# Opening loads, block-sum scalings and a row-factor power in another order

## The chip, the cores and the metric

The kernel runs on one core of one Trainium2 chip. The metric is the device time of one execution in microseconds (us), the median of several runs. TensorE (PE in the profile, its weight loads PEld) multiplies, VectorE (DVE), ScalarE (ACT) and GpSimd (POOL) work elementwise, SyncE (SP) and ScalarE issue the DMA transfers. Every engine takes its own instructions strictly in the order in which they were recorded and waits on semaphores for the others.

## The reference

One layer of a hybrid decoder trunk over 2048 positions and 16 meta tokens, 1024 channels wide. Everything is float32:

```python
h = concat([meta, x])                      # (1, 16 + 2048, 1024)
hn = rms_norm(h, norm1_g)                  # h * rsqrt(mean(h*h) + EPS) * g
proj = einsum('bld,de->ble', hn, w_in)     # 1024 -> 8 x 512
cx, cb, cc, cg, q, k, v, rg = split(proj, 8)
conv_out = short_conv_branch(cx, cb, cc, conv_w) * silu(cg)
ret = head_group_norm(retention_chunkwise(rotary(q), rotary(k), v), ret_norm_g)
mixed = concat([conv_out, ret * silu(rg)])
out = rms_norm(h + einsum('ble,ed->bld', mixed, w_out), final_g)[:, 16:]
```

The large work is the projection with w_in (1024 by 4096) and the one with w_out (1024 by 1024).

## The kernel before

**Tiling.** Positions are taken in two rounds (r = 0, 1) of 1024. A round's x stands transposed in 16 tiles of 128 channels by 512 positions, named by k (0 to 7, eight slices of channels) and j (0, 1, two halves of the positions). Eight units follow each other in a round: four convolution groups and four retention heads, each with two sets of four weight tiles ("ra", 128x512 each).

**Split products.** A float32 operand is split into a high part (rounded to a short float32 form) and a low part (the rest): ScalarE writes the high part (`mh` of a tile of x, `wh` of a weight tile), VectorE subtracts it for the low part (`ml`, `wl`). A product is three matmuls of 512 columns: high by high, high by low, low by high. `split` (line 107) does it; with a gain factor ScalarE's line is L113 and VectorE's L114, without it L110 and L122.

**Seven products for eight.** Most units use a scheme with seven block products (`quad`, L232): the weights go in as sums of the four blocks (`stationary`, line 134, whose sums GpSimd makes: L119, L122, L122, L149), x as sums of its four blocks (`block_sums`, line 177: L188 on ScalarE scales x tiles by the gain in place, L185 on VectorE, L122 on GpSimd). The first unit runs before these sums exist, so it multiplies plainly (`quad_plain`, L289), a contraction step k at a time: six matmuls for each tile of x (two weight tiles by three parts), with weight tiles 0 and 2 for k = 0 to 3 and tiles 1 and 3 for k = 4 to 7.

**The opening.** ScalarE's queue loads the gain and a first piece (128 of 512 columns, all that step k = 0 needs) of weight tiles 0 and 2 (L927). SP's queue loads x tile 0, then the remaining 384 columns of both weight tiles (L975), then x tiles 1 to 3, weight tiles 1 and 3, and the rest of x. Ten warm-up matmuls (L941) run before the first product. `begin` (line 968) splits the pieces (L984, L985).

**The row factors.** The norm's factor of each position is a power of the row's mean square: 16 half-row tiles are loaded (L363), ScalarE squares and sums them (L403), VectorE makes the variance (L119, L302), GpSimd raises it to -1/2 (`rsqrt_mean`, L305), VectorE puts it on a diagonal (L310), and TensorE spreads it over partitions (L336). This happens for the 512 positions of j = 0 and again for those of j = 1 while the first unit runs. Its results scale the first unit's outputs (L530).

**What sets the order.** The framework takes the program as written, estimates times, and records each engine's instructions in the order in which its estimate starts them. `tc.issue_after(ins)` keeps what stands inside from being recorded ahead of `ins`. Tiles come from rings of slots ("ra": 8), and a load waits until its slot is free. A DMA's landing is told on one of eight semaphores in turn, so a ninth transfer is issued when the first has landed.

Of the kernel before, what the change touches and what calls it, by code (L numbers as in the profile page):

```python
# [78 lines left out]
def hybrid_trunk(ctx: ExitStack, tc: tile.TileContext, t, out: bass.AP, chunk_decay):  # L79
# [27 lines left out]
    def split(hi, lo, src, scale=None, eng=nc.vector):  # L107

        if scale is None:
            nc.scalar.copy(out=hi, in_=src)  # L110
            sub(eng, lo, src, hi.bitcast(F32))
            return
        nc.scalar.mul(hi, src, scale)  # L113
        nc.vector.scalar_tensor_tensor(  # L114
            out=lo, in0=src, scalar=scale, in1=hi.bitcast(F32), op0=ALU.mult, op1=ALU.subtract
        )
# [14 lines left out]

    summed = [None]

    def stationary(blocks):
# [10 lines left out]
        w = [parts(a11), parts(a12)]  # L145
        add(nc.gpsimd, s1, a21, a22)
        sub(nc.gpsimd, a21, a11, a21)
# [14 lines left out]

    def moving(load, scale=None, after={}):


        m = [[] for _ in range(8)]
        blocks = []
        for j in range(2):
            for half in range(2):
                for kt in range(KH):  # L170
                    k = half * KH + kt
                    blocks.append(load(k, j))
                    parts(m, BLOCK[half][j], kt, blocks[-1], scale(k) if scale else None)
                    after.get((j, k), lambda: None)()
        return m, blocks
# [122 lines left out]
    def rsqrt_mean(r, total):  # L298

        n, w = total.shape  # L300
        v = small.tile([P, CH], F32, name="rs_v", tag="rs_v", bufs=4)
        nc.vector.tensor_scalar(  # L302
            out=v[:n, :w], in0=total, scalar1=1.0 / D, scalar2=EPS, op0=ALU.mult, op1=ALU.add
        )
        nc.gpsimd.tensor_tensor(out=r, in0=v[:n, :w], in1=neg_half[:n, :w], op=ALU.pow)  # L305
        return v[:n, :w]
# [106 lines left out]
    def load_x(r):  # L413
        def load(k, j):
            a = gen("x")[:, :HB]
            nc.sync.dma_start(a, t["xT"][r, j, k])
            return a
# [273 lines left out]
    def head(h, r, m, rot_t, f, turning, blocks, ahead, sums, first=(), between=((), idle, idle)):  # L691
# [5 lines left out]
        k, v, late = [None, None], [None, None], []  # L697
        rot = meta_table(h) if blocks[1] else None
        tables = [rot_t[:, :, j * HB : (j + 1) * HB] for j in range(2)]
# [225 lines left out]
    opening = {n: raw() for n in (0, 2)}  # L925
    for n, a in opening.items():
        nc.scalar.dma_start(a[:, PIECES[0]], t["w_in"][2 * NG, n][:, PIECES[0]])  # L927
    make_identity(nc, ident)
# [27 lines left out]
    for r in range(NR):  # L956
# [7 lines left out]
        if r == 0:  # L964
            w = [None] * 4
            loads = w_loads(2 * NG)

            def begin(half):
                if half:
                    for n in (1, 3):  # L970
                        w[n] = plain_part(n, loads[n], FIRST_W)
                    return
                for n, a in opening.items():
                    w[n] = a, operand(FIRST_W, n)
                    nc.sync.dma_start(a[:, PIECES[1]], t["w_in"][2 * NG, n][:, PIECES[1]])  # L975
                done = []
                for cs in PIECES:
                    with ExitStack() as behind:
                        for ins in done:
                            behind.enter_context(tc.issue_after(ins.ins))  # L980
                        for n, a in opening.items():
                            hi, lo = w[n][1]
                            done = [
                                nc.scalar.copy(out=hi[:, cs], in_=a[:, cs]),  # L984
                                nc.vector.tensor_tensor(  # L985
                                    out=lo[:, cs], in0=a[:, cs], in1=hi[:, cs].bitcast(F32), op=ALU.subtract
                                ),
                            ]

            m, b = moving(  # L990
                load_x(r), gain_of, {(0, 0): lambda: begin(0), (0, KH - 1): lambda: begin(1), (0, KT - 1): normalise_meta}
            )
            first = [[p for a, p in w]]
            blocks = None, meta_products([a for a, p in w])
            first.append(plain_parts(w_loads(2 * NG + 1)))
            load_tables()
            nc.sync.dma_start(cols, t["cols"])
            t3 = [a[:, i * HB : (i + 1) * HB] for a in (row_tile("t3", 1) for _ in range(2)) for i in range(2)]
            t1 = [brief("t1") if n < BRIEF else sb.tile([P, HB], F32, name="t1", tag="tc", bufs=COPIES) for n in range(KH)]
            for kt in range(KH):  # L1000
                b11, b21, b12, b22 = (b[n * KH + kt] for n in range(4))
                block_sums(b11, b12, b22, b21, t1[kt], t3[kt], gain_of(kt), gain_of(KH + kt), nc.gpsimd)
                parts(m, 2, kt, b22)
                parts(m, 6, kt, b21)
            for _ in row_factors(0, f):
                pass
            nc.sync.dma_start(causal, t["causal"])
            nc.sync.dma_start(conv_w, t["conv_w"])
            nc.sync.dma_start(ret_g, t["ret_norm_g"])

# [93 lines left out]
```

## Time and profile before

| | |
|---|---|
| median of 3 runs | 871.72 us (871.09 to 872.45) |
| profiled execution, device time | 872.54 us |
| its span, first to last instruction | 870.7 us |
| instructions in the trace | 12707 |
| granted TensorE clock | 0.999 |
| bytes read from HBM, written | 90.91 MB, 25.17 MB |

Times in the trace count from the first instruction. A row of the timeline has a start, a duration, engine, line, operation, tiles written and read, shape, a count where equal instructions follow each other, and in brackets how long the engine was idle before it and what ended that. A row of the table by stretches has, for each engine, busy us and the number of instructions, then the granted clock, the share of the DMA engines and GB/s. Durations of neighbours overlap by about 0.1 us on ScalarE and VectorE, because they are pipelined.

### The profile page before, as it was taken

To read this page: it belongs to the slowest core of one execution; us is meant where nothing else is said; L and a number is where in the kernel's file an instruction comes from. 1 tells how busy PE (TensorE), PEld (TensorE's weight loads), DVE (VectorE), ACT (ScalarE), POOL (GpSimd) and SP (SyncE) were. 2 spreads that over 40 slices of the span, in tenths; PEclk is the share of its full clock that TensorE was granted. 3 is DMA by queue.
4 is the path that set the end of the run, shared out by engine and by line. 5 is a ranking of instruction groups with operands and counts; after the bars stand their busy time and mean duration, and the time that the engine had idled before them with its cause. 6 is when DMAs were issued, how large, how long until landed. Compare 5 with 4: busy or idle time off the path is not lost.

```text
span 870.7 us, 12707 instructions
## 1 busy us (share of the span) xinstructions
PE 856.9 (98%) x4216; PEld 704.6 (81%) x4216; DVE 707.0 (81%) x1194; ACT 498.5 (57%) x899; POOL 395.0 (45%) x286
## 2 busy tenths in 40 slices
PE   8999999999999999999999999999999999999996
PEld 6878887878787878788888888888888887888885
DVE  6889988888897977989789898988767799655553
ACT  8675548383845554848383747553333565555553
POOL 0653332322246644352233333355746555677773
PEclk9999999999999999999999999999999999999999
DMA  9624236373656633845254645637122583555431
GB/s 332 224 81 97 74 78 166 105 174 107 136 194 184 202 98 97 311 150 145 61 137 141 130 161 121 206 109 218 49 77 81 179 317 133 168 171 175 152 134 73
DMA packets 127218, 129.51 MB, mean 149 GB/s; under 512 B 58352, under 2 KB 75568, under 8 KB 127152
## 3 DMA queue, kind: packets, MB, share of 16 engines
q1 hardware_dynamic: 126576, 128.30, 49.2%
q8 instruction: 33, 0.54, 0.3%
q10 hardware_dynamic: 576, 0.40, 0.1%
q14 instruction: 33, 0.27, 0.1%
HBM read 90.91 MB, written 25.17 MB: 133 GB/s over the span
## 4 chain that ended last, share of the span: by engine, by line
PE 82%; DVE 5%; ACT 4%; issue 2%; DMA 2%; SPq 0%; POOLq 0%; POOL 0%; ACTq 0%; DVEq 0%
PE pj L232 71%; PE pj L289 3%; DVE ml L122 2%; PE ms L818 2%; PE ms L807 2%; PE ms L817 2%; PE ms L794 2%; DMA t<-sums_w 1%; PE ms L452 1%; ACT wh L110 1%; DVE wl L122 1%; ACT v L762 1%; ACT v L765 1%; ACT tc L239 1%; DMA x<-in_xT 1%
## 5 line engine op out<-in xcount | busy, mean ns | idle before, releaser
L232 PE MATMUL pj<-mh,wl 128*128 128x512 f32 x1008 | 397.0, 394 | 2.6 <-ACT tc L239 2.5
L232 PE MATMUL pj<-mh,wh 128*128 128x512 f32 x1008 | 393.0, 390 | 0.0
L232 PE MATMUL pj<-ml,wh 128*128 128x512 f32 x1008 | 392.8, 390 | 0.0
L110 ACT CAST wh<-ra 128x512 fp32r<-128x512 f32 x216 | 133.8, 620 | 249.4 <-PE pj L232 199.6
L122 DVE TENSOR_TENSOR wl<-ra,wh 128x512 fp32r<-128x512 f32 x216 | 190.1, 881 | 45.7 <-ACT wh L110 43.9
L232 PEld LDWEIGHTS pj<-mh,wl 128*128 128x128 f32 x1008 | 189.3, 188 | 46.3 <-ACT tc L239 5.5
L232 PEld LDWEIGHTS pj<-mh,wh 128*128 128x128 f32 x1008 | 189.2, 188 | 39.6
L232 PEld LDWEIGHTS pj<-ml,wh 128*128 128x128 f32 x1008 | 189.4, 188 | 37.7
L119 POOL TENSOR_TENSOR sa<-ra 128x512 f32<-128x512 f32 x36 | 52.6, 1460 | 99.3 <-DMA ra<-in_w_in 34.3
L122 POOL TENSOR_TENSOR ra<-sa,ra 128x512 f32<-128x512 f32 x36 | 53.0, 1472 | 91.8 <-DVE wl L122 88.8
L149 POOL TENSOR_TENSOR ra<-ra 128x512 f32<-128x512 f32 x36 | 60.2, 1672 | 48.4 <-issue 38.5
L122 POOL TENSOR_TENSOR ra<-ra 128x512 f32<-128x512 f32 x36 | 56.9, 1580 | 50.2 <-PE ms L452 27.9
L239 ACT COPY tc<-pj 128x512 f32<-128x512 f32 x108 | 62.7, 581 | 0.1
L289 PE MATMUL pj<-mh,mh 128*128 128x512 f32 x128 | 50.7, 397 | 1.2 <-ACT mh L113 0.7
L289 PE MATMUL pj<-mh,ml 128*128 128x512 f32 x128 | 50.0, 390 | 1.0 <-DVE ml L122 1.0
L289 PE MATMUL pj<-ml,mh 128*128 128x512 f32 x128 | 48.0, 392 | 0.0
L887 DVE TENSOR_TENSOR yo<-pj,yo 128x512 f32<-128x512 f32 (+1 forms) x33 | 22.1, 674 | 31.8 <-PE pj L232 23.4
L592 POOL TENSOR_TENSOR c<-c,rr 128x512 f32<-128x512 f32 x14 | 25.5, 1820 | 25.6 <-DVE c L633 16.9
L830 POOL TENSOR_TENSOR rp<-rs,neg_half 128x4 f32<-128x4 f32 x16 | 18.9, 1184 | 39.2 <-DVE rs L119 39.1
L893 POOL TENSOR_TENSOR z<-yo,final_g 128x512 f32<-128x512 f32 x16 | 26.9, 1680 | 18.5 <-DVE yo L887 18.5
L110 ACT CAST wh<-sa 128x512 fp32r<-128x512 f32 x36 | 22.3, 619 | 18.1 <-PE pj L232 17.7
L119 POOL TENSOR_TENSOR yo<-yo,tc 128x512 f32<-128x512 f32 x18 | 28.6, 1589 | 8.8 <-ACT tc L239 8.8
(151 smaller groups left out, 1202.6 us busy)
## 6 DMA issues: line engine op xcount, KB each, us to landing
ra<-in_w_in SPq DMA_DIRECT2D x126, 256.0 KB, 2.8
x<-in_xT SPq DMA_DIRECT2D x48, 256.0 KB, 4.9
w<-in_w_out SPq DMA_DIRECT2D x32, 256.0 KB, 4.3
ra<-mixed SPq DMA_DIRECT2D x32, 256.0 KB, 2.7
yo<-in_x SPq DMA_DIRECT2D x32, 256.0 KB, 4.9
ra<-in_x SPq DMA_DIRECT2D x16, 256.0 KB, 3.4
mixed<-c SPq DMA_DIRECT2D x16, 256.0 KB, 2.5
mixed<-qg SPq DMA_DIRECT2D x16, 256.0 KB, 2.4
```

What stands on the lines that cost most here:

```text
L110: nc.scalar.copy(out=hi, in_=src)
L119: eng.tensor_tensor(out=out, in0=a, in1=b, op=ALU.add)
L122: eng.tensor_tensor(out=out, in0=a, in1=b, op=ALU.subtract)
L149: summed[0] = nc.gpsimd.tensor_tensor(out=a12, in0=a12, in1=a11, op=ALU.subtract)
L232: nc.tensor.matmul(bank, a[:, ks], b, start=first and kt == 0 and n == 0, stop=kt == KH - 1 and n == 2, skip_group_check=not first,)
L239: copied[0] = nc.scalar.copy(out=c, in_=bank)
L289: nc.tensor.matmul(banks[i], a[:, ks], b, start=half + kt + n == 0, stop=half == 1 and kt == KH - 1 and n == 2,)
L592: eng.tensor_tensor(out=out, in0=a, in1=b, op=ALU.mult)
L794: nc.tensor.matmul(up[:, cs], kd[:, cs], vj[:, cs], start=True, stop=True)
L830: nc.gpsimd.tensor_tensor(out=rp, in0=rs, in1=neg_half.rearrange("p (c a) -> p c a", a=1), op=ALU.pow)
L887: last[0] = nc.vector.tensor_tensor(out=y[:, cs], in0=pp[:, cs], in1=y[:, cs], op=ALU.add)
L893: nc.gpsimd.tensor_tensor(out=ys[i][j], in0=y, in1=final_g[:, j * HB : (j + 1) * HB], op=ALU.mult)
```

## The change

The change has four parts. (1) The first piece of weight tile 2 moves from ScalarE's queue to SP's, right behind x tile 0, then comes x tile 1, then the rest of both weight tiles; the splits of these pieces are ordered between those of x tiles 0, 1 and 2. (2) The block sums are recorded only after the split of x tile 7, so the scalings of x tiles 0 to 3 (L188, now L194) move behind it. (3) Later loads and the meta table are ordered behind the x loads. (4) In the first call of `stationary`, the weight sum on GpSimd is ordered behind the row-factor power of j = 1.

```diff
-        nc.scalar.mul(hi, src, scale)
+        scaled[0] = nc.scalar.mul(hi, src, scale)
...
         w = [parts(a11), parts(a12)]
-        add(nc.gpsimd, s1, a21, a22)
+        with tc.issue_after(powered.pop().ins) if powered else nullcontext():
+            add(nc.gpsimd, s1, a21, a22)
...
-    def moving(load, scale=None, after={}):
+    def moving(load, scale=None, after={}, behind={}):
...
-                    blocks.append(load(k, j))
-                    parts(m, BLOCK[half][j], kt, blocks[-1], scale(k) if scale else None)
+                    with ExitStack() as order:
+                        for ins in behind.get((j, k), lambda: ())():
+                            order.enter_context(tc.issue_after(ins.ins))
+                        blocks.append(load(k, j))
+                        parts(m, BLOCK[half][j], kt, blocks[-1], scale(k) if scale else None)
...
-        nc.gpsimd.tensor_tensor(out=r, in0=v[:n, :w], in1=neg_half[:n, :w], op=ALU.pow)
+        power = nc.gpsimd.tensor_tensor(out=r, in0=v[:n, :w], in1=neg_half[:n, :w], op=ALU.pow)
+        if n == P and w == CH and len(powers) < NR:
+            powers.append(power)
+            powered[:] = [power]
...
-    for n, a in opening.items():
-        nc.scalar.dma_start(a[:, PIECES[0]], t["w_in"][2 * NG, n][:, PIECES[0]])
+    nc.scalar.dma_start(opening[0][:, PIECES[0]], t["w_in"][2 * NG, 0][:, PIECES[0]])
...
+            def piece(at):
+                cs = PIECES[at]
                 for n, a in opening.items():
+                    if n or at:
+                        with tc.issue_after(fetched[0].ins):
+                            fetched[0] = nc.sync.dma_start(a[:, cs], t["w_in"][2 * NG, n][:, cs])
+                with tc.issue_after(scaled[0].ins):
+                    for n, a in opening.items():
...
+                        cast = nc.scalar.copy(out=hi[:, cs], in_=a[:, cs])
...
+            after = {
+                (0, 0): lambda: pieces.append(piece(0)),
+                (0, 1): lambda: pieces.append(piece(1)),
+                (0, KH - 1): rest_of_tiles,
+                (0, KT - 1): lambda: (pieces.append(scaled[0]), meta_behind()),
+            }
+            m, b = moving(load_x(r), gain_of, after, {(0, 1): lambda: pieces[0], (0, 2): lambda: pieces[1]})
...
+                    with tc.issue_after(pieces[2].ins):
+                        block_sums(b11, b12, b22, b21, t1[kt], t3[kt], gain_of(kt), gain_of(KH + kt), nc.gpsimd)
```

What it makes of the recorded order is shown at three places. In names, `mh00` to `mh03` and `mh10` to `mh13` are the high parts of x tiles 0 to 7, `mh20` to `mh23` those of the first set's weight tiles 0 to 3.

ScalarE at the start, before, from the first split on:

```order
L113 ACTIVATE mh00_123<-x_121,gain_69 128x512
L984 CAST mh20_127<-ra_94 128x128
L984 CAST mh22_130<-ra_95 128x128
L984 CAST mh20_127<-ra_94 128x384
L984 CAST mh22_130<-ra_95 128x384
L188 ACTIVATE x_121<-x_121,gain_69 128x512
L113 ACTIVATE mh01_143<-x_141,gain_69 128x512
L113 ACTIVATE mh02_149<-x_147,gain_69 128x512
L113 ACTIVATE mh03_155<-x_153,gain_69 128x512
L110 CAST mh21_161<-ra_159 128x512
L188 ACTIVATE x_141<-x_141,gain_69 128x512
```

The same place after the change, with the first piece of tile 2 now on SP's queue:

```order
L113 ACTIVATE mh00_122<-x_120,gain_69 128x512
L992 CAST mh22_131<-ra_95 128x128
L992 CAST mh20_127<-ra_94 128x128
L113 ACTIVATE mh01_137<-x_135,gain_69 128x512
L992 CAST mh20_127<-ra_94 128x384
L992 CAST mh22_131<-ra_95 128x384
L113 ACTIVATE mh02_149<-x_147,gain_69 128x512
L113 ACTIVATE mh03_155<-x_153,gain_69 128x512
L110 CAST mh21_161<-ra_159 128x512
L110 CAST mh23_167<-ra_165 128x512
L113 ACTIVATE mh10_173<-x_171,gain_69 128x512
```

Tile 1's split has moved ahead of the weights' rest, and no L188 stands among the splits; all four come behind `mh13`.

GpSimd around the second 128x4 power, before:

```order
L122 TENSOR_TENSOR t3_315<-x_254,x_147 128x512
L122 TENSOR_TENSOR t3_315<-x_260,x_153 128x512
L119 TENSOR_TENSOR sa_747<-ra_717,ra_719 128x512
L305 TENSOR_TENSOR rc_442<-rs_v_443,neg_half_73 128x4
L122 TENSOR_TENSOR ra_717<-ra_713,ra_717 128x512
```

and after:

```order
L122 TENSOR_TENSOR t3_315<-x_254,x_147 128x512
L122 TENSOR_TENSOR t3_315<-x_260,x_153 128x512
L311 TENSOR_TENSOR rc_442<-rs_v_443,neg_half_73 128x4
L119 TENSOR_TENSOR sa_747<-ra_717,ra_719 128x512
L122 TENSOR_TENSOR ra_717<-ra_713,ra_717 128x512
```

The power (L305, now L311) and the sum of two weight tiles have changed places.

VectorE around the diagonal that waits for this power (L310), before; `wl_749` and `wl_753` are low parts of the next unit's first two weight tiles, `ml63` belongs to the block sums:

```order
L122 TENSOR_TENSOR ml62_356<-x_183,mh62_355 128x512
L302 TENSOR_SCALAR rs_v_443<-ss_420 128x4
L122 TENSOR_TENSOR wl_749<-ra_713,wh_748 128x512
L383 TENSOR_TENSOR ev_456<-cols_75,rs_v_443 128x16
L122 TENSOR_TENSOR wl_753<-ra_715,wh_752 128x512
L122 TENSOR_TENSOR ml63_369<-x_189,mh63_368 128x512
L310 TENSOR_TENSOR rot_446<-ident_70,rc_442 128x512
L374 TENSOR_TENSOR rc2_452<-rc_442 128x4
```

and after:

```order
L308 TENSOR_SCALAR rs_v_443<-ss_420 128x4
L392 TENSOR_TENSOR ev_456<-cols_75,rs_v_443 128x16
L122 TENSOR_TENSOR ml62_356<-x_183,mh62_355 128x512
L319 TENSOR_TENSOR rot_446<-ident_70,rc_442 128x512
L383 TENSOR_TENSOR rc2_452<-rc_442 128x4
L122 TENSOR_TENSOR wl_749<-ra_713,wh_748 128x512
L122 TENSOR_TENSOR ml40_698<-t3_314,mh40_697 128x512
L385 TENSOR_TENSOR vk_454<-cols_75,rc2_452 128x16
L122 TENSOR_TENSOR wl_753<-ra_715,wh_752 128x512
L122 TENSOR_TENSOR ml63_369<-x_189,mh63_368 128x512
```

The diagonal (now L319) has moved ahead of both weight subtractions and of `ml63`. Behind these rows the order on VectorE, ScalarE and GpSimd is the same in both kernels as far as the weight pair that the prediction ends at, and from there on.

75 lines of the change are left out of this document (34 added, 41 removed).

## The prediction

> **What bounds the kernel now.** I read the page's busy shares first, then the chain that ended last by engine, then the table of busy time in stretches of 5 us, then TensorE's waits in the first 130 us.
>
> ```profile
> PE 856.9 (98%) x4216; PEld 704.6 (81%) x4216; DVE 707.0 (81%) x1194; ACT 498.5 (57%) x899; POOL 395.0 (45%) x286
> PE 82%; DVE 5%; ACT 4%; issue 2%; DMA 2%; SPq 0%; POOLq 0%; POOL 0%; ACTq 0%; DVEq 0%
> ...
> 0.00:5.00 5.00, 4.01 (x11) 1.53 (x11) 0.70 (x3) 2.44 (x4) 0.78 (x8) 1.00 0.60 188
> 5.00:10.00 5.00, 3.80 (x16) 2.57 (x15) 3.91 (x9) 4.47 (x9) 0.00 (x0) 1.00 0.91 329
> 10.00:15.00 5.00, 5.00 (x37) 3.77 (x35) 3.71 (x8) 5.00 (x10) 0.00 (x0) 1.00 1.06 394
> ...
> 50.00:55.00 5.00, 4.15 (x44) 2.53 (x43) 4.07 (x9) 4.33 (x11) 1.80 (x2) 1.00 0.00 0
> 55.00:60.00 5.00, 5.00 (x23) 4.12 (x23) 5.00 (x7) 1.73 (x5) 4.84 (x3) 1.00 0.00 0
> 60.00:65.00 5.00, 4.90 (x22) 3.76 (x22) 5.00 (x7) 3.10 (x6) 3.32 (x4) 1.00 0.19 51
> ...
> PE ms L336 <- DVE rot L310: 0.8, 1, 0.8
> PE pj L289 <- ACT mh L113: 0.7, 1, 0.7
> PE pj L289 <- ACT mh L984: 0.6, 1, 0.6
> ```
>
> TensorE is busy 98% of the span, so only its holes are worth anything, and the change touches the first 63 us. There it stands still at three places: 1.2 us in 5 to 10 us (waits of 0.6 and 0.7 for ScalarE), 0.8 us at 52 us (waits for VectorE's L310), and 0.1 us in 60 to 65 us. In that last stretch VectorE is full (5.00 of 5.00), and from 55 us on. Keep this: there are two clocks running side by side, and the later one counts.
>
> **The opening.** Engine rows in order of time:
>
> ```profile
> 4.81 0.52 PE L289 MATMUL pj<-mh,mh 128*128 128x512 f32 x1
> ...
> 5.53 1.13 ACT L984 CAST mh<-ra 128x128 fp32r<-128x128 f32 x3 [0.77 <-DMA ra<-in_w_in]
> ...
> 5.88 0.50 PE L289 MATMUL pj<-mh,mh 128*128 128x512 f32 x1 [0.55 <-ACT mh L984]
> ...
> 6.56 0.72 ACT L188 ACTIVATE x<-x,gain 128x512 f32<-128x512 f32 x1
> ...
> 7.19 1.93 ACT L113 ACTIVATE mh<-x,gain 128x512 fp32r<-128x512 f32 x3
> ...
> 7.95 0.50 PE L289 MATMUL pj<-mh,mh 128*128 128x512 f32 x1 [0.65 <-ACT mh L113]
> ...
> 10.67 0.72 ACT L188 ACTIVATE x<-x,gain 128x512 f32<-128x512 f32 x1
> ...
> 11.30 0.71 ACT L113 ACTIVATE mh<-x,gain 128x512 fp32r<-128x512 f32 x1
> ...
> 12.06 0.19 PEld L289 LDWEIGHTS pj<-mh,mh 128*128 128x128 f32 x1 [0.15 <-ACT mh L113]
> ...
> x<-in_xT SPq DMA_DIRECT2D x1, 256.0 KB, 5.6
> ...
> 57.27 5.44 PE pj L232 x24
> ```
>
> A contraction step k is six L289 products, 0.227 us apart (24 of the same shape take 5.44 us in the chain's piece at 57.27), so 1.36 us. Before: step 0 begins at 4.81, step 1 at 7.95, step 4 at 12.06. The change lets the second weight's first piece land beside the first's, so the wait at 5.88 should go; it takes the four block-sum scalings (L188, 0.72 each) from between the splits and puts them behind x tile 7; and it puts x tile 1 ahead of the weights' rest. Without the scaling at 6.56, tile 1's split starts by 6.56 and step 1 by 7.3 even if nothing landed earlier; with the earlier landing, about 6.3. Added: one issue of 64 KB on SP, taken from ScalarE's queue; the bytes in front of every later tile are the same.
>
> But step 4 needs x tile 4. Its load is issued at 5.13 (the row is the DMA view's, for the stretch from 5.0 to 5.3 us) and lands 5.6 us later, at 10.7; the split takes 0.71, so step 4 cannot begin before about 11.5, against 12.06. **Term: 0.5 us**, bounds 0 (a landing 0.5 later) and 0.6. The other 1.1 us won before it turn into a new wait in front of step 4. From there the moved scalings stand behind tile 7, at 13.4 (four splits 0.64 apart from 10.8) to 16.0 on ScalarE, and tile 8 is split at 16.0 to 16.7, while TensorE comes to it at 11.5 + 4 x 1.36 = 16.9. This cover is 0.2 us thick; without it TensorE waits as much as it is short, and the slack found below takes that up.
>
> **The power ahead of the weight sum.** Rows of the second place:
>
> ```profile
> 24.37 13.91 SPq L363 DMA_DIRECT2D ra<-in_x  x16
> ...
> 44.55 0.63 ACT L403 ACTIVATE ra<-ra 128x512 f32<-128x512 f32 x1
> ...
> 36.52 1.03 POOL L305 TENSOR_TENSOR rc<-rs_v,neg_half 128x4 f32<-128x4 f32 x1 [4.40 <-DVE rs_v L302]
> ...
> 46.43 0.16 DVE L302 TENSOR_SCALAR rs_v<-ss 128x4 f32<-128x4 f32 x1
> ...
> 48.52 1.29 POOL L119 TENSOR_TENSOR sa<-ra 128x512 f32<-128x512 f32 x1 [3.45 <-PE pj L289]
> 49.78 1.48 POOL L305 TENSOR_TENSOR rc<-rs_v,neg_half 128x4 f32<-128x4 f32 x1
> ...
> 51.29 0.69 DVE L310 TENSOR_TENSOR rot<-ident,rc 128x512 f32<-128x512 f32 x1 [0.93 <-POOL rc L305]
> ...
> 50.80 0.39 PE L289 MATMUL pj<-ml,mh 128*128 128x512 f32 x1
> 52.04 0.70 PE L336 MATMUL ms<-rot,ones 128*128 128x512 f32 x1 [0.85 <-DVE rot L310]
> ...
> 62.33 0.39 PE L232 MATMUL pj<-mh,wh 128*128 128x512 f32 x1
> 62.81 0.47 PE L232 MATMUL pj<-mh,wl 128*128 128x512 f32 x1
> ```
>
> The variance is ready at 46.6, yet the power starts at 49.78, because the sum ahead of it in GpSimd's queue waits until 48.52. TensorE issues its last product at 50.80 and is free at 51.03; it gets L336 at 52.04: **1.0 us** lost. In the new order the power runs at about 46.6. (The last square, at 44.55, moves one or two places of some 0.6 us back on ScalarE, to about 45.4, but the variance no longer stands behind a 0.6 us split of VectorE, so I keep 46.4.) The power takes 1.03 to 1.48 us (its two 128x4 instances, at 36.52 and 49.78), L310 starts at 47.7 to 48.1, and L336 is ready before TensorE comes to it. That wait is gone.
>
> TensorE alone would then reach its product with the third weight pair (62.81) earlier by 0.5 + 1.0 + 0.25 (the hole in front of 62.81: the last issue is 62.33, the next was due at 62.56) = **1.75 us**, at 61.05.
>
> **What is late next.** That product reads a low part that VectorE makes last:
>
> ```profile
> 51.29:62.67 11.38, 11.38 (x17) 1.00 0.00 0
> ...
> 48.63 1.74 DVE L122 TENSOR_TENSOR ml<-x,mh 128x512 fp32r<-128x512 f32 x1 [0.31 <-ACT mh L110]
> ...
> 53.87 3.09 DVE L122 TENSOR_TENSOR ml<-t,mh 128x512 fp32r<-128x512 f32 x5
> ...
> 54.45 3.66 POOL L122 TENSOR_TENSOR ra<-ra 128x512 f32<-128x512 f32 x1 [3.20 <-DVE u L530]
> 56.88 0.15 DVE L491 COPY carry<-ms 128x2 f32<-128x2 f32 x1
> 56.95 1.72 DVE L530 TENSOR_TENSOR u<-u,rr 128x512 f32<-128x512 f32 x1
> ...
> 61.99 0.68 DVE L122 TENSOR_TENSOR wl<-ra,wh 128x512 fp32r<-128x512 f32 x1
> ```
>
> From L310 to the end of that subtraction VectorE has no idle time: 11.38 busy of 11.38. In the new order L310 goes ahead of two weight subtractions and a tile's (the order on VectorE, above), 3 x 0.61 us (five take 3.09) = 1.83 more behind it. A GpSimd add that gets its operands in between stretches the VectorE instruction beside it by 1.05 to 1.1 us (1.74 at 48.63, 1.72 at 56.95, where 0.6 to 0.7 is usual); back-to-back subtractions keep it out instead (3.66 at 54.45, let in at the small copy at 56.88). In the new order the weight sum becomes ready at about 48.5, when VectorE has just started its closed run. If it is kept out until the copy, three stretches remain in the run as before (11.38 + 1.83 = 13.2): from 47.7 to 48.1 the subtraction ends at 60.9 to 61.3 and TensorE goes on at 61.05 to 61.4. **Shift 1.4 to 1.75; I take 1.5**, since the row at 54.45 shows the same situation. If it gets in at once, 1.1 more: 62.0 to 62.4, shift 0.3 to 0.7.
>
> The Trainium skill bears on this in "SBUF — State Buffer", section "SBUF: two separate sides": the port pair that VectorE and GpSimd share is an exclusive lock held for a whole instruction, taken by whichever starts first. Read as a hand-over after each instruction, it gives the second case; the trace agrees on the exclusion, but at 54.45 GpSimd waited through five instructions, not one.
>
> Behind 62.81 the order of all engines is as before, and waits there are relative to what TensorE and VectorE have done, so the shift stays until the end.
>
> **Sum.** The profiled execution is 872.54 us (span 870.7 and 1.8 around it), 0.8 above the median 871.72 and just outside the three runs. 872.54 - 1.5 = 871.0; from the median it would be 870.2. If some of that 0.8 is in the stall at 52 us, there is less to win in other runs; no row tells, so I go halfway: **870.6 us**.
>
> **Rivals.**
> - The sum gets in at once (shift 0.3 to 0.7): 871.0 to 872.2. For it: 48.63; against it: 54.45. Chance 0.28.
> - TensorE's full 1.75, from the median: 869.9. For it: VectorE's early estimate (60.9) lies under 61.05. Against: the closed run leaves 0.1 us. Chance 0.20.
> - Slower: the power late. L310 now stands in front of the two weight subtractions, and the first product with them waits if the power does. The power hangs on 16 loads of rows (L363, from 24.37 on), whose slots are freed by VectorE and ScalarE work that the change reorders. Each us of lateness beyond a power ending at 49.5 (62.67 less 13.2) is a us lost; with it ending at 51.4 the time is 873.5. That asks for the last square 3.3 us later than 45.4; the order moves it by about 0.9. Chance 0.07.
> - The forecast itself, shift 1.4 to 1.7, from the median or from the profiled time: 870.0 to 871.1. Chance 0.45.
>
> **Range and chances.** 0.2% is 1.74 us, about what a measurement of this kernel can tell from no change: below 869.98 is faster, above 873.46 slower. The range runs from 869.2 (full shift, a run at the low end) to 872.2 (the sum gets in at once). Faster 0.25 (the full shift and the lower end of the forecast), same 0.68, slower 0.07.
>
> **What would show it.** Right: no wait at 5.88; step 4 at about 11.5 with a new wait in front of it; the power at 46 to 47 on GpSimd ahead of the sum; L336 without a wait; and a larger wait than 0.1 in front of the third weight pair's product, ended by VectorE, at 61 to 61.5. Wrong: step 4 earlier than 11.3 (tile 4 landed earlier), the power later than 48, VectorE idle inside the run after L310, or a new wait behind 63 us.

## The result, and the profile after

| | median of 13 runs | profiled execution | its span |
|---|---|---|---|
| kernel before | 872.24 us (871.09 to 874.87) | 872.54 us | 870.7 us |
| changed kernel | 874.79 us (872.91 to 877.05) | 874.20 us | 872.4 us |

The ratio is 1.0027, with a 95% interval of 1.0019 to 1.0035: the change makes the kernel about 2.4 us slower. Forecast was 870.6, with 0.07 for slower.

TensorE's waits between 4 and 70 us of the changed kernel (operation, what it waited for, total, times, longest):

```profile
PE pj L238 <- DVE wl L122: 2.6, 1, 2.6
PE pj L295 <- ACT mh L992: 0.6, 2, 0.4
```

Lines have moved: L289 is now L295, L232 is L238, L310 is L319, L336 is L345, L305 is L311, L403 is L412, L530 is L539. The wait for the diagonal is gone from this execution, as was wanted. In its place stands one of 2.6 us for VectorE at the third weight pair. Rows in order of time around it:

```profile
45.49 0.61 ACT L110 CAST mh<-x 128x512 fp32r<-128x512 f32 x1
46.12 0.59 ACT L553 COPY cb<-pj 128x512 f32<-128x512 f32 x1
46.60 0.63 ACT L412 ACTIVATE ra<-ra 128x512 f32<-128x512 f32 x1
...
47.87 1.57 POOL L311 TENSOR_TENSOR rc<-rs_v,neg_half 128x4 f32<-128x4 f32 x1 [2.79 <-DVE rs_v L308]
49.76 1.54 POOL L119 TENSOR_TENSOR sa<-ra 128x512 f32<-128x512 f32 x1 [0.32 <-DMA ra<-in_w_in]
52.64 1.74 POOL L122 TENSOR_TENSOR ra<-ra 128x512 f32<-128x512 f32 x1 [1.33 <-DVE vk L385]
...
49.48 0.69 DVE L319 TENSOR_TENSOR rot<-ident,rc 128x512 f32<-128x512 f32 x1 [0.92 <-POOL rc L311]
50.08 1.24 DVE L383 TENSOR_TENSOR rc<-rc 128x4 f32<-128x4 f32 x1
...
53.14 1.79 DVE L122 TENSOR_TENSOR ml<-x,mh 128x512 fp32r<-128x512 f32 x1
54.85 1.78 DVE L539 TENSOR_TENSOR cb<-cb,rr 128x512 f32<-128x512 f32 x1
56.55 1.79 DVE L539 TENSOR_TENSOR u<-u,rr 128x512 f32<-128x512 f32 x1
58.26 3.09 DVE L122 TENSOR_TENSOR ml<-t,mh 128x512 fp32r<-128x512 f32 x5
...
63.14 0.68 DVE L122 TENSOR_TENSOR wl<-ra,wh 128x512 fp32r<-128x512 f32 x1
...
60.96 0.39 PE L238 MATMUL pj<-mh,wh 128*128 128x512 f32 x1
63.97 0.47 PE L238 MATMUL pj<-mh,wl 128*128 128x512 f32 x1 [2.62 <-DVE wl L122]
```

Read it from the end. TensorE came 1.37 us earlier than before (last issue at 60.96 instead of 62.33), but goes on 1.16 later (63.97 instead of 62.81), 0.14 after VectorE's low part. That low part is the last of a closed run which starts with the diagonal at 49.48 and has no hole, by VectorE's busy time in that stretch:

```profile
49.48:63.83 14.35, 14.35 (x20) 1.00 0.01 5
```

It was 11.38 before. Four of its instructions are stretched, one for each weight sum of GpSimd (a 128x4 one to 1.24 by the sum at 49.76; three to 1.79 by the others); before there were three. The diagonal itself waits 0.92 for the power, which starts late since the last square stands at 46.60: the copy of a product at 46.12 and a split are ahead of it on ScalarE, though the last row had landed at 45.43. That landing is itself late. The load of the last row, from the view of the tile `ra`, before and after (its duration in ns and its start, then the us from its issue to its landing):

```profile
L363 SPq DMA_DIRECT2D ra<-in_x x1: 382/382/382, 37.9 to 37.9; - x1
DMA to landing us min/median/max: 6.2/6.2/6.2
...
L372 SPq DMA_DIRECT2D ra<-in_x x1: 382/382/382, 39.4 to 39.4; - x1
DMA to landing us min/median/max: 6.0/6.0/6.0
```

Issued at 37.91 and 39.42, the row landed at 44.08 before and at 45.43 now, and its square followed 0.47 and 1.17 us behind. So of the 2.05 us by which the square is later (44.55 and 46.60), 1.35 come from the load and 0.7 from the order on ScalarE.

Of the 1.7 us between the two spans, 1.16 to 1.2 are there from 64 us on, 0.36 come at 297 us (a wait of 0.2 for VectorE and a slower restart), 0.1 at 742 us. The medians lie 2.55 apart, so some 0.8 us of that is not in this pair of profiles.

### The profile page after: what moved, and what is told of

It is laid out like the page before. It is cut to its first block, busy times and chain, and to the rows that moved or that the text cites. A ratio compares the mean times of both kernels' runs of the same rounds, so it can differ in the third digit from the quotient of the medians.

```text
span 872.4 us, 12711 instructions
## 1 busy us (share of the span) xinstructions
PE 857.2 (98%) x4216; PEld 704.5 (81%) x4216; DVE 708.2 (81%) x1194; ACT 498.8 (57%) x899; POOL 397.0 (46%) x286
## 3 DMA queue, kind: packets, MB, share of 16 engines
q1 hardware_dynamic: 126720, 128.37, 49.5%
## 4 chain that ended last, share of the span: by engine, by line
PE 85%; DVE 5%; ACT 4%; DMA 3%; issue 2%; POOL 0%; SPq 0%; POOLq 0%; ACTq 0%; DVEq 0%
PE pj L238 71%; PE pj L295 6%; PE ms L828 2%; PE ms L817 2%; PE ms L827 2%; PE ms L804 2%; DVE ml L122 1%; DMA ra<-in_x 1%; DVE wl L122 1%; PE ms L461 1%; DMA ra<-in_w_in 1%; ACT wh L110 1%; DVE ml L114 1%; ACT v L775 1%; ACT v L772 1%
## 5 line engine op out<-in xcount | busy, mean ns | idle before, releaser
L238 PE MATMUL pj<-mh,wl 128*128 128x512 f32 x1008 | 397.2, 394 | 5.4 <-DVE wl L122 2.8
L238 PE MATMUL pj<-mh,wh 128*128 128x512 f32 x1008 | 393.0, 390 | 0.0
L238 PE MATMUL pj<-ml,wh 128*128 128x512 f32 x1008 | 392.8, 390 | 0.0
L238 PEld LDWEIGHTS pj<-mh,wl 128*128 128x128 f32 x1008 | 189.3, 188 | 49.3 <-ACT tc L245 5.1
L238 PEld LDWEIGHTS pj<-mh,wh 128*128 128x128 f32 x1008 | 189.2, 188 | 39.7
L238 PEld LDWEIGHTS pj<-ml,wh 128*128 128x128 f32 x1008 | 189.3, 188 | 37.8
L119 POOL TENSOR_TENSOR sa<-ra 128x512 f32<-128x512 f32 x36 | 52.9, 1470 | 93.9 <-DMA ra<-in_w_in 38.2
L152 POOL TENSOR_TENSOR ra<-ra 128x512 f32<-128x512 f32 x36 | 60.2, 1672 | 48.8 <-issue 38.8
L122 POOL TENSOR_TENSOR ra<-ra 128x512 f32<-128x512 f32 x36 | 55.0, 1529 | 48.7 <-PE ms L461 28.0
L295 PE MATMUL pj<-mh,ml 128*128 128x512 f32 x128 | 50.2, 392 | 1.0 <-DVE ml L122 1.0
L295 PE MATMUL pj<-mh,mh 128*128 128x512 f32 x128 | 49.7, 392 | 0.7 <-ACT mh L992 0.6
L295 PE MATMUL pj<-ml,mh 128*128 128x512 f32 x128 | 48.2, 396 | 0.0
L119 POOL TENSOR_TENSOR yo<-yo,tc 128x512 f32<-128x512 f32 x18 | 28.8, 1602 | 9.2 <-ACT tc L245 9.2
L601 POOL TENSOR_TENSOR c<-c,tc 128x512 f32<-128x512 f32 x14 | 24.2, 1726 | 19.4 <-ACT tc L627 17.9
```

Of the source, the lines that this page charges most:

```text
L119: eng.tensor_tensor(out=out, in0=a, in1=b, op=ALU.add)
L122: eng.tensor_tensor(out=out, in0=a, in1=b, op=ALU.subtract)
L152: summed[0] = nc.gpsimd.tensor_tensor(out=a12, in0=a12, in1=a11, op=ALU.subtract)
L238: nc.tensor.matmul(bank, a[:, ks], b, start=first and kt == 0 and n == 0, stop=kt == KH - 1 and n == 2, skip_group_check=not first,)
L295: nc.tensor.matmul(banks[i], a[:, ks], b, start=half + kt + n == 0, stop=half == 1 and kt == KH - 1 and n == 2,)
L601: eng.tensor_tensor(out=out, in0=a, in1=b, op=ALU.mult)
```

## The experiments

Sixteen runs were made, each beside the kernel before on the same chip (e13 to e16 are one execution each). One fact needs no run: with the other parts in place, the recorded order of every engine is the same, row by row, **with part 4 and without it**. The hold of part 2 alone already puts the power ahead of the sum in the order by estimates. So the changed kernel consists of the opening loads (parts 1 and 3) and the hold (part 2); the order of power and sum is a consequence.

The first table has the medians, as measured against the kernel before on the same chip:

| kernel | us | before | ratio, 95% interval |
|---|---|---|---|
| e1, swap alone | 871.69 | 872.49 | 0.9994 (0.9985 to 1.0003) |
| e11, swap alone again | 871.97 | 872.08 | 1.0001 (0.9993 to 1.0010) |
| e10, opening loads alone | 872.85 | 872.08 | 1.0010 (1.0001 to 1.0020) |
| e2, loads and swap, no hold | 872.23 | 872.49 | 1.0000 (0.9990 to 1.0010) |
| e9, hold alone | 873.63 | 872.08 | 1.0013 (1.0003 to 1.0023) |
| e12, changed kernel again | 874.05 | 872.08 | 1.0023 (1.0012 to 1.0034) |
| e3, changed, late subtractions | 872.92 | 872.49 | 1.0008 (0.9999 to 1.0017) |
| e4, swap, late subtractions | 871.85 | 872.49 | 0.9993 (0.9984 to 1.0002) |
| e7, no hold, late subtractions | 872.00 | 871.93 | 0.9997 (0.9988 to 1.0007) |
| e5, no hold, third pair put back | 872.61 | 871.93 | 1.0003 (0.9995 to 1.0012) |
| e6, changed, three sums | 874.07 | 871.93 | 1.0020 (1.0009 to 1.0031) |
| e8, changed, rest pieces first | 875.82 | 871.93 | 1.0042 (1.0030 to 1.0053) |

The second has the marks of profiled executions of both kernels and of the single parts, taken from the rows of each timeline: start of the last row square, end of the power, start of the diagonal, length from there to the end of the third pair's low part, start of the third pair's product.

| execution | own time | square | power | diagonal | run | third pair |
|---|---|---|---|---|---|---|
| before | 872.54 | 44.55 | 51.26 | 51.29 | 11.38 | 62.81 |
| before, second (e15) | 871.64 | 43.61 | 49.81 | 49.84 | 11.37 | 61.45 |
| changed | 874.20 | 46.60 | 49.44 | 49.48 | 14.35 | 63.97 |
| changed, second (e12) | 873.79 | 46.23 | 49.07 | 49.11 | 14.24 | 63.49 |
| changed, third (e16) | 873.31 | 45.81 | 48.65 | 48.68 | 14.25 | 63.08 |
| hold alone (e9) | 872.07 | 44.70 | 46.98 | 47.87 | 13.68 | 61.70 |
| hold alone (e13) | 871.79 | 44.64 | 46.93 | 48.93 | 12.56 | 61.63 |
| hold alone (e14) | 873.31 | 44.71 | 47.56 | 47.90 | 13.74 | 61.79 |
| loads alone (e10) | 872.56 | 44.58 | 50.58 | 50.61 | 11.98 | 62.74 |
| swap alone (e1) | 871.42 | 43.70 | 47.47 | 47.50 | 12.12 | 61.55 |
| swap alone (e11) | 870.92 | 43.92 | 47.43 | 47.48 | 11.92 | 61.03 |
| loads and swap (e2) | 874.16 | 44.09 | 47.37 | 47.40 | 12.74 | 62.06 |

### The parts one by one

Swap alone (e1, e11): the kernel before, and

```diff
-        add(nc.gpsimd, s1, a21, a22)
+        with tc.issue_after(powered.pop().ins) if powered else nullcontext():
+            add(nc.gpsimd, s1, a21, a22)
```

> The kernel before, with part 4 alone: the power of j = 1 stands ahead of the weight sum on GpSimd; loads, scalings and the opening stay as before. Theory A (the swap is worth what was predicted, the opening parts spoil it by making the last row square and so the power late): last square at 44.6 and variance at 46.4 as before, power over at about 48.1, VectorE's diagonal at 48.3 instead of 51.29, no wait of TensorE at L336's line, and the third weight pair's product starts at 61.3 to 61.7 instead of 62.81, since VectorE's list has the pair's low part two subtractions earlier. Time 1.1 to 1.5 us under the kernel before: 870.7 to 871.2 against 872.24. Theory B (the swap itself costs it: the weight sum now runs beside VectorE's closed run, whoever loads what): the third pair's product at 63 or later, time 872.2 to 874.8.

Rows of e1, from GpSimd, VectorE and TensorE:

```profile
46.14 1.33 POOL L308 TENSOR_TENSOR rc<-rs_v,neg_half 128x4 f32<-128x4 f32 x1 [1.45 <-DVE rs_v L305]
47.43 1.30 POOL L119 TENSOR_TENSOR sa<-ra 128x512 f32<-128x512 f32 x1
...
47.50 1.77 DVE L316 TENSOR_TENSOR rot<-ident,rc 128x512 f32<-128x512 f32 x1 [0.19 <-POOL rc L308]
...
61.55 0.50 PE L235 MATMUL pj<-mh,wl 128*128 128x512 f32 x1 [0.19 <-ACT tc L242]
```

The third pair comes where theory A has it, 1.26 us ahead of the first execution of before; power and diagonal come 0.6 and 0.8 sooner than A has them, since the last square stands at 43.70. But the second execution of before has its third pair at 61.45 without the swap. The median is only 0.8 better, where A had 1.1 to 1.5, and its interval holds no change.

> The swap alone once more, beside the others on one chip, for its size: by the first run 0.5 to 1.1 us under the kernel before; third pair's product at 61.3 to 62.0.

The second run had a profiled execution with the third pair at 61.03 and no wait, yet a median only 0.1 below before (0.5 to 1.1 expected); that execution was the fastest of its twelve. So the swap is worth between nothing and 1 us, not the 1.2 of one profile against one profile.

The changed kernel without the hold (e2):

```diff
-                    with tc.issue_after(pieces[2].ins):
+                    with nullcontext():
```

> The changed kernel without part 2: the block sums are not held behind the split of x tile 7, the opening loads stay as changed. Theory A1 (the hold of the scalings makes the row stage late): the last row square goes back from 46.60 to about 44.6 to 45.5, the power is over by 48.3, the third pair's product starts at 61.3 to 62.5 and the time is 870.7 to 872.3. Theory A2 (the opening loads or the extra order behind the x loads make it late): the last square stays at 46.4 or later, and only the two places by which VectorE's list has the third pair's low part earlier are gained, 1.2 us: 873.3 to 873.8.

The last square goes back to 44.09, the power is over at 47.37, the median is that of before: A1, and the opening loads do not make the row stage (squares, variance and power) late by themselves. The third pair comes at 62.06, not for VectorE, which has its low part at 60.14, but for ScalarE. Rows of e2, from GpSimd, ScalarE, VectorE and TensorE:

```profile
51.80 4.73 POOL L122 TENSOR_TENSOR ra<-ra 128x512 f32<-128x512 f32 x1 [2.54 <-DVE cb L539]
56.61 1.61 POOL L122 TENSOR_TENSOR ra<-sa,ra 128x512 f32<-128x512 f32 x1
...
58.25 0.62 ACT L110 CAST wh<-ra 128x512 fp32r<-128x512 f32 x1 [4.30 <-POOL ra L122]
...
61.42 0.59 ACT L245 COPY tc<-pj 128x512 f32<-128x512 f32 x1
...
58.90 1.24 DVE L122 TENSOR_TENSOR wl<-ra,wh 128x512 fp32r<-128x512 f32 x1 [1.83 <-ACT wh L110]
...
62.06 0.50 PE L238 MATMUL pj<-mh,wl 128*128 128x512 f32 x1 [0.87 <-ACT tc L245]
```

GpSimd's second sum took 4.73 us, kept out by back-to-back VectorE instructions, ScalarE stood 4.30 us in front of the high part made from the third, and the copy of the bank into which the third pair's product is added is the sixth instruction behind that. In this execution, with VectorE early enough, this second chain sets when the third pair starts.

Opening loads alone (e10): the same edit, and

```diff
-        with tc.issue_after(powered.pop().ins) if powered else nullcontext():
-            add(nc.gpsimd, s1, a21, a22)
+        add(nc.gpsimd, s1, a21, a22)
```

> The changed kernel without the hold and without the order of power and sum: the opening loads, their splits and the order behind the x loads alone. GpSimd's list has the sum ahead of the power as in the kernel before. Theory A: row stage and third pair as before (last square 44.1 to 45.1, power over at 50.5 to 51.5, third pair's product at 62.4 to 63.0), opening no earlier (TensorE without a pause from 7.8 to 8.1), time within 0.6 us of the kernel before. Theory E (the loads make something late): 1 us or more over it.

Row stage and third pair are as in before (44.58, 62.74); the median is 0.8 over before, a little more than expected, with an interval that just leaves out no change. Its profiled execution (872.56) does not show where.

Hold alone (e9): the kernel before, and

```diff
-                block_sums(b11, b12, b22, b21, t1[kt], t3[kt], gain_of(kt), gain_of(KH + kt), nc.gpsimd)
+                with tc.issue_after(held_back[0].ins):
+                    block_sums(b11, b12, b22, b21, t1[kt], t3[kt], gain_of(kt), gain_of(KH + kt), nc.gpsimd)
```

with `held_back` set to the split of x tile 7.

> The kernel before with part 2 alone: the block sums are recorded behind the split of x tile 7; loads as before, no order written for the power. The recorded list of GpSimd then has the power ahead of the weight sum all the same. Theory A (the hold is what makes the row stage late, and with it VectorE's run): last row square at 46.3 to 47.2 instead of 44.55, power over at 49.2 to 50.2, no wait at L336's line or a small one, the third pair's product at 63.2 to 64.4 behind a wait for VectorE of 1.5 us or more; time 1.2 to 2.6 us over the kernel before on this chip. Theory E (it takes the changed opening loads as well): last square by 45.2, time within 0.7 us of the kernel before.

The median agrees with A (1.55 us over before), the profiled execution with E: last square at 44.70, third pair at 61.70. Two more were looked at, with one more of each kernel.

> The hold alone, a second profiled execution. Theory A (the hold is enough): last row square at 46.0 or later, power over at 48.8 or later, third pair's product at 63.0 to 64.4. Theory E (only with the changed loads): last square by 45.2, third pair's product by 62.5; then the 1.55 us of its median stay without a place.

> The hold alone, a third profiled execution; as for the second.

> The kernel before, a second profiled execution, as a measure of how far executions of one kernel differ: last square between 43.7 and 45.1, third pair's product at 62.3 to 63.0 behind the wait at L336's line.

> The changed kernel, a third profiled execution: last square between 46.0 and 47.2, third pair's product between 63.4 and 64.6, by either way that GpSimd's second sum goes (in at once, or starved until VectorE's list runs dry).

E holds: with the loads of before, the hold leaves the last square at 44.6 to 44.7 in all three. Without the hold, the changed loads leave it at 44.1 to 45.1 (e2, e10, e5, e7). Only both together make it late: 45.81 to 47.17 in five executions with the list of the changed kernel here (the three in the table, 46.37 in e3, 47.17 in e6). The looks at single executions also show how far these differ: e15 and e16 came sooner than expected, e16 with its last square at 45.81 and its third pair at 63.08.

Two things make the square late. One is the order: with the loads of before ScalarE has the last square ahead of the copy, here in e9,

```profile
44.19 0.61 ACT L110 CAST mh<-x 128x512 fp32r<-128x512 f32 x1
44.70 0.63 ACT L403 ACTIVATE ra<-ra 128x512 f32<-128x512 f32 x1
...
45.44 0.59 ACT L544 COPY cb<-pj 128x512 f32<-128x512 f32 x1
```

and the changed kernel has it behind (46.12, then 46.60). The square stands 1.1 to 1.4 us behind the landing of its row in those five executions, 0.5 to 1.0 in the seven that have only the hold or only the loads. The other is the landing: 44.7 to 46.1 in the five, 43.7 to 44.2 with the hold alone and 43.6 to 44.6 with the changed loads and no hold. The first of the 16 row loads is already issued later there (at 24.6 to 25.8, in the seven at 23.7 to 24.4); why was not followed up. The 0.36 us at 297 us is in every execution with the hold whose VectorE list was not touched, in none without it. The rest of the hold's 1.55 us has no place in its three profiles and stays open; the profiled execution of e9 was the fastest of its eleven, so it need not show what the median has.

The second look at before is as telling. Rows of e15, from GpSimd, VectorE and TensorE:

```profile
46.77 1.59 POOL L119 TENSOR_TENSOR sa<-ra 128x512 f32<-128x512 f32 x1 [2.18 <-DMA ra<-in_w_in]
48.32 1.49 POOL L305 TENSOR_TENSOR rc<-rs_v,neg_half 128x4 f32<-128x4 f32 x1
...
49.84 0.69 DVE L310 TENSOR_TENSOR rot<-ident,rc 128x512 f32<-128x512 f32 x1 [0.93 <-POOL rc L305]
...
51.04 1.02 PE L336 MATMUL ms<-rot,ones 128*128 128x512 f32 x2
```

The sum got its weights 1.75 us sooner than in the first (it starts at 46.77, not 48.52), the power stood 1.46 sooner, and TensorE did not wait at L336 at all. The hole that the prediction meant to close is not in every execution.

> The changed kernel on the same chip as the three runs of single parts: 2.0 to 3.0 us over the kernel before, third pair's product at 63.7 to 64.6 behind a wait of 2 us or more. If the parts add up as theory A has it, it lies within 0.8 us of the hold alone; the swap adds nothing to it, since the recorded order is the same without it.

Slightly under what was expected: 1.97 over before, third pair 63.49 behind 1.4 us of waiting. The hold alone (1.55) and the loads alone (0.77) add up to 2.3, near the 1.97 and 2.55 of the changed kernel. And in this execution GpSimd went the other way. Rows of e12, from GpSimd, VectorE and TensorE:

```profile
53.34 5.46 POOL L122 TENSOR_TENSOR ra<-ra 128x512 f32<-128x512 f32 x1 [3.02 <-DVE wl L122]
...
49.11 1.76 DVE L319 TENSOR_TENSOR rot<-ident,rc 128x512 f32<-128x512 f32 x1 [0.91 <-POOL rc L311]
...
57.64 1.71 DVE L539 TENSOR_TENSOR u<-u,rr 128x512 f32<-128x512 f32 x1
59.27 1.77 DVE L539 TENSOR_TENSOR cb<-cb,rr 128x512 f32<-128x512 f32 x1
60.97 1.78 DVE L122 TENSOR_TENSOR ml<-t,mh 128x512 fp32r<-128x512 f32 x1
```

The second sum took 5.46 us instead of 1.74, and still four VectorE instructions are stretched; the run is 14.24 instead of 14.35.

### VectorE's list and its price

Late subtractions (e3; e4 and e7 have the same edit on e1 and e2): in `stationary`, the four splits for the fifth product come behind the fourth pair's.

```diff
-        return w + [parts(a) for a in (a11, s1, a21, a12, a22)]
+        w += [parts(a11), parts(s1)]
+        if late:
+            with tc.issue_after(subbed[0].ins):
+                late.pop()()
+        return w + [parts(a) for a in (a21, a12, a22)]
```

> The changed kernel; on VectorE alone, the four subtractions for the fifth product's x sums move from ahead of the third weight pair's low part to behind the fourth pair's. Theory A (TensorE waits for the place of that subtraction in VectorE's list, not for the data): GpSimd's chain still ends at 57.8, the low part ends four subtractions earlier, 63.83 less 4 x 0.61 is 61.4, the third pair's product starts at 61.5 instead of 63.97, no new wait at the fifth product (its four are over at about 65.2, it starts at 66.9), time 2.0 to 2.5 us under the changed kernel: 872.3 to 872.8. Theory C (VectorE's total work up to there is what counts, the wait only moves to the next product): 0.5 us gained or less, 874.3 or more, with a wait at the fourth or fifth product.

The low part is over at 61.19, the third pair starts at 61.83 without a wait, and no wait follows at the fourth, fifth and seventh product; one of 0.4 us for ScalarE inside the sixth, at 82 us, is new. The changed kernel lies 2.55 and 1.97 over before in its two measurements, this one 0.43, so it is 1.5 to 2.1 us better: A in kind, with a gain from below its range (2.0 to 2.5) to its lower end.

> The kernel before with part 4 alone and the same four subtractions moved behind the fourth pair's low part. Theory A: TensorE waits neither at L336's line nor at the third pair, the whole shift of 1.75 us shows: 870.4 to 870.7, 0.3 us or more under the swap alone. Theory C: the same time as the swap alone, within 0.3 us.

> The changed kernel without the hold, and with the four subtractions of the fifth product moved behind the fourth pair's low part: both causes taken away. Theory A: the third pair's low part is over by 60.2, TensorE reaches it at 60.9 to 61.1 without a wait, 1.7 ahead of the kernel before, and the shift holds to the end: 870.6 to 871.2. Theory C (what is saved here is waited for at a later product, as the swap with the same move showed no gain over the swap alone): 871.7 to 872.4, with a new wait at the fourth to seventh product.

Here the edit gives nothing that can be measured (e4 is 0.16 us slower than e1, e7 0.07 over before): theory C in its result, though not in its way, since no new wait shows at the fourth to seventh product. In both, TensorE reaches the third pair without a wait, at 61.40 and 61.78 (e7 behind one of 0.4 at its L349, with the last square at 45.07): its own way there is what is left.

The place of the low part (e5): e2, with the third pair's split ordered behind that of the sixth x sum (`late` holds its subtraction).

```diff
+        with tc.issue_after(late.pop().ins) if late else nullcontext():
+            w.append(parts(a11))
-        return w + [parts(a) for a in (a11, s1, a21, a12, a22)]
+        return w + [parts(a) for a in (s1, a21, a12, a22)]
```

> The changed kernel without the hold of the block sums (as e2), and the third pair's low part put back to the place that VectorE's list has it in the changed kernel, two instructions later; nothing else differs from e2. Theory A (the place in VectorE's list is a cause by itself, beside the late rows): row stage as in e2 (last square about 44.1, power over at 47.4), third pair's product 2 x 0.6 later than e2's 62.06, so 63.1 to 63.3, time 1.0 to 1.2 us over e2: 873.2 to 873.5. If the late rows alone were the cause, it would equal e2: 872.0 to 872.5.

The third pair comes at 63.03 and the median is 0.9 worse than e2's, each against its own before: close to A. But VectorE is not full there. Rows of e5:

```profile
56.33 1.71 DVE L541 TENSOR_TENSOR u<-u,rr 128x512 f32<-128x512 f32 x1
60.48 0.69 DVE L541 TENSOR_TENSOR cb<-cb,rr 128x512 f32<-128x512 f32 x1 [2.44 <-ACT cb L555]
```

It idles 2.44 us, for a copy that ScalarE makes behind the high part for which GpSimd was late (4.86 us for its second sum): the chain of e2 again. Place and chain cannot be parted here.

One sum fewer (e6; it leaves out the fourth weight sum of the first set, so its result is another one):

```diff
-        summed[0] = nc.gpsimd.tensor_tensor(out=a12, in0=a12, in1=a11, op=ALU.subtract)
+        if not first:
+            summed[0] = nc.gpsimd.tensor_tensor(out=a12, in0=a12, in1=a11, op=ALU.subtract)
```

> The changed kernel with the fourth weight sum on GpSimd left out in the first set of the seven-product scheme (the last pair's weights enter unsummed, so part of the first head's projection is another value); VectorE's list is unchanged. Theory A (each GpSimd operation that gets in beside VectorE's closed run costs VectorE 1.1 us, 1.79 against 0.68): one stretched instruction fewer, the third pair's low part ends at 62.7 instead of 63.83, its product starts at 62.9, time 873.4 to 873.9. Theory D (the stretch has another cause, or is made up elsewhere in the run): four instructions stay stretched or the run ends within 0.3 of 63.83, time 874.5 to 875.1.

The row stage was late by another 0.6 in this execution, so the run is to be read, not the time. The third pair's product, at 64.14, waits 1.17 us for a copy of ScalarE. VectorE's busy time in the run:

```profile
50.05:63.18 13.13, 13.13 (x20) 1.00 0.01 2
```

13.13 without a hole and three stretched instructions, against 14.35 and 14.24 with four: this GpSimd operation inside the run cost VectorE 1.1 to 1.2 us. The time, 2.14 over before, is not told from the changed kernel's.

Rest pieces first (e8):

```diff
-                (0, 0): lambda: pieces.append(piece(0)),
-                (0, 1): lambda: pieces.append(piece(1)),
+                (0, 0): lambda: (pieces.append(piece(0)), pieces.append(piece(1))),
```

> The changed kernel with x tile 1 loaded, and its split placed, behind the rest pieces of both weight tiles instead of ahead of them. What the opening is bound by: if by the bytes that step 1 needs (x tiles 0 and 1 and both weight tiles, in whatever order), the last of the four lands at 7.2 to 7.6 all the same and TensorE runs without a pause from 7.8 to 8.1 as in both kernels (7.96 and 7.95). If by the place of the rest piece of weight tile 2 (landed at 7.37), it now lands at 6.2 to 6.7 and TensorE runs without a pause from 7.0 to 7.4. Time: within 1 us of the changed kernel by either, since VectorE's list behind it changes in some places too.

The first of the two holds: the last of the four landed at 7.30 (now x tile 1; 7.37 in the changed kernel, the rest of weight tile 2), and TensorE runs without a pause from 8.10. It is not the bytes alone, though: in the kernel before the same four had landed at 6.25. The time is worse than expected by either theory (3.9 us over before): row stage and run are later still (48.03, third pair at 65.30), and in its profiled execution the clock fell, below.

## Why the prediction was wrong

- **The opening, 0.5 us: measured 0.2.** The wait at 5.88 went, as forecast. But the first product of step 4 started at 11.96, against 12.16 before (the 12.06 of the prediction is the row of its weight load), not at 11.5, and there was no new wait ahead of it. The step that failed is "step 1 by 7.3 even if nothing landed earlier": it looked at x tile 1 and forgot that step 1 also reads the weights' rest, which the change puts behind that tile. ScalarE's row in the changed kernel says so,

```profile
7.39 0.51 ACT L992 CAST mh<-ra 128x384 fp32r<-128x384 f32 x1 [0.40 <-DMA ra<-in_w_in]
```

  and TensorE flows from 7.96 (7.95 before). e8 shows that turning the two round gains nothing. The new order of loads even brings the last of what step 1 reads later: at 7.37 instead of 6.25, and at 6.6 to 8.1 in the nine executions with these loads, 5.8 to 6.7 in the eight with the loads of before. Step 4 started at 11.5 to 12.7 in the nine and at 11.5 to 12.2 in the eight, so a gain is not shown.
- **The swap takes the wait at L336 away: right in kind.** L345 stood at 50.26, 1.78 earlier than before; 0.45 of that is order, since 14 products of the first unit follow it and 12 did before. At its last product ahead of the third pair's low part TensorE was 1.37 earlier (60.96), where the forecast had 1.5, the terms of 0.5 and 1.0. In the second and third execution 0.9 and 0.3 us of wait were left. And the wait itself was a property of one execution: e15 has none. The size of 1.0 was read from a single draw; the prediction named the doubt ("no row tells") and split the difference in the time, but kept the term whole.
- **The last square at 45.4: it came at 46.60.** This is the step that cost most. The prediction moved the square by "one or two places of some 0.6 us" on ScalarE and put the landing of its row at no change, without a reason. The places held, with 0.7; the landing came 1.35 later (45.43, not 44.08). The rival "the power late" names these 16 loads, but the forecast has no term for them. The step from the square to the variance was right (1.0 forecast, 46.60 to 47.56 measured). With the variance so late (46.4 kept, 47.56 measured) and a power of 1.57 beside a VectorE split, the diagonal started at 49.48 instead of 47.7 to 48.1: **1.4 to 1.8 us**.
- **VectorE's run of 13.2: it took 14.35.** The three subtractions more were right (1.83). The failed step is "if it is kept out until the copy, three stretches remain": the weight sum comes ready just as the diagonal starts, gets in at once in all three executions of the changed kernel, and is a fourth stretch inside the run, **1.1 us** (e6). The row at 54.45, from which the prediction took the opposite, concerns the sum after it, and e12 shows that being kept out spares nothing: the starved operation stretches its instruction later.
- **The rivals were priced apart and came together.** "The power late" was neutral up to a power ending at 49.5 with a run of 13.2; it ended at 49.44. "The sum gets in" cost 1.1. Diagonal at 49.48 plus 14.35 is 63.83, 2.7 us past the forecast 60.9 to 61.3, and the sign turns. Both came with the same reordering in all three executions, so keeping their chances apart left out the case that came.
- **The shift stays to the end: nearly.** 1.16 at 64 us became 1.7. Of that 0.36 comes from 284 us, where VectorE starts its L119 at 284.43, behind a ScalarE copy for which it does not wait in the kernel before (282.84 there); the recorded order is the same in that place, and why the wait reaches further was not followed up.

Shown by the runs: the loads and the hold together make the last square late, by a later landing and one place on ScalarE, the run has a fourth stretch, and the third pair's place in VectorE's list turns that into TensorE's wait (e3 takes most of the loss back). Open: why the row loads come later, and the part of the hold's and of the loads' medians (1.2 and 0.8 us) that no profile places.

No version beats the kernel before by more than the measurement tells. The swap alone and the swap with late subtractions are the lowest, 0.1 to 0.8 us under before, with intervals that hold no change.

## What to carry to other kernels

When a wait is removed in front of one engine, add up the list of the engine that is next, from the new start and with every instruction that another engine can stretch, and take "starts later" and "takes longer" as one case if the same reordering causes both. When the order on an engine changes, follow the loads whose slots its work sets free too, and give their landing a term. A wait of 1 us seen in one profiled execution may not be in the next: look at two before it becomes a term. Before crediting an edit, compare the recorded order with and without it; here one of four parts changed nothing.

## What the hardware showed

**The granted clock fell to half for 3.4 us after a wait of about 2 us, in three executions.** TensorE by stretches of 2 us (busy, granted clock, DMA share, GB/s) in e8, where it had waited 2.1 us until 65.30:

```profile
64.00:66.00 2.00, 0.70 (x3) 1.00 0.00 0
66.00:68.00 2.00, 2.00 (x8) 0.62 0.42 132
68.00:70.00 2.00, 2.00 (x7) 0.53 0.48 130
70.00:72.00 2.00, 2.00 (x10) 1.00 0.00 0
```

Eight products were 0.427 us apart instead of 0.227, a loss of 1.6 us. The same happened once each in e2 and e4 at 742 us, behind a wait of 1.8 us; all executions wait there, for 1.3 to 1.8 us, and the others kept the full clock behind it, and so did the changed kernel behind its 2.6 us. The profiled time of e2 in the table (874.16) carries this loss.

The Trainium skill, in "TensorE: Matmul & The Clock Gate", section "Part 1: The HAM clock gate (the "warmup" mystery)", has the clock halved after an idle window of about 3.4 us that runs freely, and restored after a busy one. The length (3.4 us) and the spacing at half clock (0.427) agree with the trace; that waits of 1.8 to 2.1 us, shorter than a window, were enough three times is what the runs here add. What decides whether it happens is not shown.

**Starved or let in, GpSimd's sum cost VectorE the same.** The second weight sum took between 1.74 us (changed) and 5.46 us (e12); VectorE's run was 14.35 and 14.24. The difference lay in the chain behind it: starved, it left ScalarE idle for 4.3 us (e2).
